# The scan of a gated delta rule: odd heads moved to the other half of the partitions, and products issued one at a time

## The chip, the cores and the metric

The kernel is one launch on 1 core of a Trainium2 chip. The metric is the device time of that launch in microseconds (us). The engines are named as the profile names them: PE is TensorE, which multiplies matrices (PEld is its loading of the stationary operand), DVE is VectorE, ACT is ScalarE, POOL is GpSimd and SP is SyncE, from whose queue all transfers (DMA) are issued. SBUF is the on-chip memory of 128 partitions; PSUM is the memory that PE writes its products to.

## The reference

One transformer block in fp32 with 1024 tokens of width 1024. Its mixer has two branches. One is a gated delta rule with 4 heads of width 128; the other is a dilated attention with 8 heads of width 64. Both go through an output projection, and then a gated feed-forward layer of width 2816 follows. What the change touches is the gated delta rule, cut here to its core:

```
kb = kc * bc[..., None]                                  # 16 chunks of 64 tokens, 4 heads
a = strict_lower(kb @ kc^T * decay)
t_inv = inverse(eye + a)
u = t_inv @ (vc * bc[..., None]);  w = t_inv @ (kb * exp(gc)[..., None])
attn = (qc @ kc^T) * decay;  q_dec = qc * exp(gc)[..., None]
k_dec = kc * exp(gc[..., -1:] - gc)[..., None];  g_end = exp(gc[..., -1])
def step(state, ...):                                    # one after the other over the 16 chunks
    v_new = u_i - w_i @ state
    o_i = q_dec_i @ state + attn_i @ v_new
    state = state * g_end_i + k_dec_i^T @ v_new
```

After the scan each head's output is normalised by its root mean square and multiplied by a gate.

## The kernel before, in words

**Stages.** PE first runs the input projections (tiles `pj`, `tp`), three fp32r products for one fp32 one: weights and activations are each split into a high and a low part, and `mm3` makes high x high, high x low and low x high. In between come the preparations of the delta rule (`post_k`, `post_q`, `intra`, `post_v`, `inverse`, `solve`). From about 281 us the scan (`chain`) runs, mixed with the rest of the input projections and with the attention (tiles `pS`, `Sr`, `tp`, `ptn`, `ptf`, `pto`, `pV`). Then come the output projection (`pw`) and the feed-forward layer (`bank`), which takes the second half of the time.

**One step of the scan.** A step is one chunk of 64 tokens for all 4 heads; two chunks c = 0 and 1 share a tile of 128 tokens t. The 64 tokens of chunk c lie in partitions 64c to 64c + 63 (`nat`), and the other half of the partitions (`sw`) holds the part of the products that gives the output. A step has three blocks of products on PE, each of four matmuls (one for each head) of 128x128 by 128 columns in fp32, and between them other engines work:

- p1: `p<-state,ckq`, the keys and queries of the chunk times the state. DVE makes `R` out of the `nat` half (four SCALAR_TENSOR_TENSOR, one a head). ACT makes `o` out of the `sw` half (`chain_o1`, four ACTIVATE), on its own time. POOL multiplies the state by its decay.
- p2: `p<-R,cg`. The matrix `cg` has 128 rows, 64 of which belong to the chunk. The other 64 meet rows of `R` that were set to zero once (a memset). ACT copies the `nat` half to `vn` (64x512), DVE adds the `sw` half to `o` (64x512).
- p3: `p<-vn,ckd`, again with 64 rows of zeros in `vn`. DVE adds it to the state (128x512).

p1 and p3 share one PSUM buffer (tag p1), p2 has another. When both chunks of a tile are done, `chain_out` normalises `o` (DVE `o<-o,on_r`), PE transposes it (`otp`) and it is written to memory (`d_mix`).

**What sets the order.** Nothing runs by hand. A planner, `Weaver`, takes generators ("strands") such as `chain`, `proj_half`, `unit` (attention) and simulates the engines with costs that stand in `Op` (lines 160 to 181): a matmul goes by its columns, an ACT instruction that reads PSUM costs 60 + 0.83 per element (+ 85 for a scale by partition), a DVE instruction 65 + 1.04 per element (+ 60 for SCALAR_TENSOR_TENSOR), and a change of the rows and columns that a matmul uses costs `SWITCH` = 120 ns. It takes whatever can start first; on PE it prefers an operation whose data were ready `MARGIN` = 850 ns before (line 399). A strand that yields a list gets it issued in one piece; `mm3` yields three products at a time. `Either` lets the planner choose an engine, with a handicap `bias` for the later ones. The instruction streams so made are fixed; on the chip every engine runs its own in order and waits on semaphores.

## Time and profile before

| | us |
|---|---|
| median of 3 runs | 1240.75 |
| lowest, highest | 1238.07, 1242.44 |
| the profiled execution, its own time | 1239.4 |
| its span, from first to last instruction | 1237.6 |
| PE busy | 1214.8 (98%) |
| DVE busy | 964.9 (78%) |
| ACT busy | 570.1 (46%) |
| POOL busy | 197.2 (16%) |

A time in the profile is one execution's; 1.35 us lie between that execution and the median of the runs, and 1.8 us between its span and its time. A fp32 matmul of the program shows as two MATMUL records. [...] How fast PE goes is read from the distance between starts.

### The profile page before, as it was taken

Reading aid. Unit: us, or ns where it says so; the run is one execution under the profiler, and the core shown is the slowest. Engines: PE = TensorE matmul, PEld = TensorE weight load, DVE = VectorE, ACT = ScalarE, POOL = GpSimd, SP = SyncE. Lnnn points to the kernel's source line nnn. Section 1 sums busy time; section 2 is a strip of 40 time slices with the busy share of each in tenths; the row PEclk is TensorE's granted clock in tenths of the full one; section 3 lists DMA queues with packets and bytes.
Section 4 is the critical chain, followed back from the end, with each engine's and each line's share of the span. In section 5 each row is a group of like instructions: output and inputs, shape, how many; then the busy total and the mean of one; then the engine's idle time right before and its main releaser. Section 6 shows DMA issues by size and latency. Waiting matters only on the chain.

```text
span 1237.6 us, 19603 instructions
## 1 busy us (share of the span) xinstructions
PE 1214.8 (98%) x6783; PEld 1015.6 (82%) x6783; DVE 964.9 (78%) x1864; ACT 570.1 (46%) x1162; POOL 197.2 (16%) x165
## 2 busy tenths in 40 slices
PE   8999999999999999999999999999999999999997
PEld 7887798888888877788788888888888888888886
DVE  5689969745999887876898867876678767976886
ACT  7535432135777667654553333333333334544541
POOL 0134321111232202110211010111001100000111
PEclk9999999999999999999999999999999999999999
DMA  8754372759887668786544444313333039645335
GB/s 272 229 158 154 111 230 78 171 188 314 243 255 226 183 182 262 236 279 196 185 136 149 143 128 128 102 61 101 119 128 118 35 104 333 246 138 150 99 123 204
DMA packets 169978, 213.42 MB, mean 172 GB/s; under 512 B 32232, under 2 KB 87016, under 8 KB 169880
## 3 DMA queue, kind: packets, MB, share of 16 engines
q1 hardware_dynamic: 169880, 212.18, 54.3%
q8 instruction: 54, 0.88, 0.3%
q14 instruction: 44, 0.36, 0.1%
HBM read 149.97 MB, written 65.95 MB: 174 GB/s over the span
## 4 chain that ended last, share of the span: by engine, by line
PE 82%; DVE 6%; DMA 5%; ACT 2%; SPq 2%; issue 1%; POOL 1%; DVEq 0%; POOLq 0%; ACTq 0%
PE bank L283 49%; PE pj L283 16%; PE pw L283 6%; PE p L283 3%; PE tp L283 3%; PE pS L283 2%; SPq L283 2%; PE pm L283 2%; PE pV L283 1%; DMA xn<-in_x 1%; DMA d_bias<-d_rev 1%; DMA y<-in_w_out 1%; DMA wor<-in_w_out 1%; DVE yc L283 0%; DMA xT<-in_x_t 0%
## 5 line engine op out<-in xcount | busy, mean ns | idle before, releaser
L283 PE MATMUL pj<-hTh,w 128*128 128x512 f32 x768 | 263.7, 402 | 5.3 <-ACT hTh L283 5.3
L283 PEld LDWEIGHTS pj<-hTh,w 128*128 128x128 f32 x768 | 145.5, 190 | 36.8 <-ACT hTh L283 5.3
L283 ACT CAST wbh<-wraw 128x512 fp32r<-128x512 f32 x130 | 80.3, 622 | 197.7 <-PE bank L283 126.1
L283 PE MATMUL pj<-hTl,w 128*128 128x512 f32 x384 | 151.3, 394 | 0.0
L283 DVE TENSOR_TENSOR wbl<-wraw,wbh 128x512 fp32r<-128x512 f32 x131 | 93.8, 718 | 29.1 <-ACT wbh L283 29.0
L283 PE MATMUL bank<-views 128*128 128x512 f32 (+1 forms) x307 | 84.8, 384 | 0.0
L283 PEld LDWEIGHTS pj<-hTl,w 128*128 128x128 f32 x384 | 72.9, 190 | 12.3 <-DVE hTl L283 0.9
L283 PE MATMUL bank<-views,dah 128*128 128x512 f32 (+1 forms) x214 | 73.5, 379 | 0.0
L283 PE MATMUL bank<-dbh,views 128*128 128x512 f32 (+1 forms) x201 | 70.3, 380 | 0.0
L283 POOL TENSOR_TENSOR m<-m,m 128x512 f32<-128x512 f32 x18 | 28.3, 1575 | 252.0 <-DVE r L283 142.1
L283 PEld LDWEIGHTS bank<-views 128*128 128x128 f32 x307 | 57.5, 188 | 11.4
L283 PE MATMUL pw<-woh,mh 128*128 128x512 f32 x128 | 52.0, 406 | 0.4 <-DVE woh L283 0.4
L283 ACT CAST w<-wr 128x512 fp32r<-128x512 f32 x53 | 32.6, 619 | 40.7 <-PE pj L283 33.5
L283 PE MATMUL pw<-wol,mh 128*128 128x512 f32 x128 | 50.1, 392 | 0.7 <-DVE wol L283 0.7
L283 PE MATMUL pw<-woh,ml 128*128 128x512 f32 x128 | 50.1, 392 | 0.0
L283 PE MATMUL bank<-dbh,dah 128*128 128x512 f32 (+1 forms) x129 | 49.1, 381 | 0.0
L283 DVE SCALAR_TENSOR_TENSOR yc<-raw,convw,yc 128x1024 f32<-128x1024 f32 x36 | 47.2, 1312 | 0.4
L283 ACT ACTIVATE Sr<-Sr,mx 128x384 f32<-128x384 f32 (+2 forms) x64 | 38.2, 598 | 19.7 <-DVE mx L283 19.4
L283 PEld LDWEIGHTS bank<-views,dah 128*128 128x128 f32 x214 | 40.0, 188 | 7.7
L283 DVE TENSOR_TENSOR m<-bank,m 128x512 f32<-128x512 f32 x44 | 30.1, 685 | 18.3 <-PE bank L283 18.3
L283 PEld LDWEIGHTS bank<-dbh,views 128*128 128x128 f32 x201 | 37.7, 188 | 7.1
L283 ACT CAST dbh<-db 128x512 fp32r<-128x512 f32 x37 | 23.0, 621 | 40.2 <-DVE db L283 22.4
(403 smaller groups left out, 3287.8 us busy)
## 6 DMA issues: line engine op xcount, KB each, us to landing
wr<-in_w_in SPq DMA_DIRECT2D x56, 256.0 KB
wraw<-in_w_gate SPq DMA_DIRECT2D x52, 256.0 KB
wraw<-in_w_up SPq DMA_DIRECT2D x52, 256.0 KB
views<-d_hid SPq DMA_DIRECT2D x47, 256.0 KB
db<-in_w_down SPq DMA_DIRECT2D x40, 256.0 KB
qs<-d_q SPq DMA_DIRECT2D x64, 128.0 KB
da<-d_hid SPq DMA_DIRECT2D x30, 256.0 KB
d_hid<-x SPq DMA_DIRECT2D x22, 256.0 KB
```

What stands on the lines that cost most here:

```text
L283: op.fn(*op.args, **op.kw)
```

## The change

Four things are done.

**Odd heads change halves.** For heads 1 and 3 the chunk's tokens are kept in the other half of the partitions: keys and queries are stored with the two chunks exchanged (`chunks_of`), `ckd`, `cbv` and `cg` are written to memory by two transfers instead of one (`store`; 8 more transfers in all), and the factors by token (`nbeg`, `egsw`) are exchanged for odd heads by one more small matmul, one ACTIVATE and one COPY. In a step, even heads then use partitions 64c and on, odd heads the other ones.

**Products with 64 rows.** p2 and p3 take only the 64 rows that count: `gg[nat[h % 2], h, :]` and `kd[nat[h % 2], h, :]`, so that heads 0 and 2 use one half of PE's rows and heads 1 and 3 the other. Even heads write one PSUM buffer, odd heads another; p2 and p3 lie in the two halves of each. The second of them is the buffer of p1 (tag p1). So `chain` now waits for `chain_o1` (priority 0 instead of 2) before it takes that buffer for p2. p1 stays as it was. The four memsets are gone. `vn`, the addition to the state and the addition to `o` are each done in two instructions of half the size, one for even and one for odd heads.

**Products singly.** `proj_half`, the output projection and the gate and up projection yield the three products of `mm3` one by one.

**POOL before DVE.** The normalisation of `o` and the sum `qf` of the attention prefer POOL; DVE gets them only where it would end more than `SPARE` = 1500 ns sooner. In the new streams POOL has all 8 of the first (none before) and 13 of 16 of the second (5 before). The planner's choices elsewhere move too: ACT has 30 instead of 22 casts to `ptf`, DVE 2 instead of 10. The planner's cost for a matmul of 64 rows to 128 columns becomes 0.87 per column (1.667 for 128 rows).

The diff, cut to its core:

```
+SPARE = 1500.0
-                c = n * 1.667 if out.shape[0] == P else ...
+                c = n * 0.87 if args[1].shape[0] == 64 and out.shape[0] == P else n * 1.667 if out.shape[0] == P else ...
...
-            yield mm3(ps[:], wh[k // 4][:, k % 4, :], wl[k // 4][:, k % 4, :], *h_of(k, hf * 512, 512),
-                      k == 0, k == KT - 1)
+            for op in mm3(ps[:], wh[k // 4][:, k % 4, :], wl[k // 4][:, k % 4, :], *h_of(k, hf * 512, 512),
+                          k == 0, k == KT - 1):
+                yield op
...
+    def store(h, dst, src):
+        if h % 2:
+            for x in (0, 64):
+                yield SY.dma_start(dst[x:x + 64], src[64 - x:128 - x])
+        else:
+            yield SY.dma_start(dst, src)
...
-        for c in range(2):
-            for z in (Rs[c], vns[c]):
-                yield G.memset(z[64 - 64 * c:128 - 64 * c, :, :], 0.0)
...
-                nat = slice(c * 64, c * 64 + 64)
-                sw = slice(64 - c * 64, 128 - c * 64)
+                nat = [slice(64 * x, 64 * x + 64) for x in (c, 1 - c)]
+                sw = nat[::-1]
...
+                    o1 = w.spawn(chain_o1(o, p1, sw, us), 0)
...
-                    w.spawn(chain_o1(o, p1, sw, us), 2)
-                p2 = yield cp.get([P, GH, P], F32, name="p2")
-                yield [mm(p2[:, h, :], gg[:, h, :], R[:, h, :]) for h in range(GH)]
+                    yield o1
+                    cp.put(p1)
+                ps = []
+                for e in range(2):
+                    z = yield cp.get([P, 2, 2, P], F32, name="p2", tag=("p2", "p1")[e])
+                    ps.append(z)
+                yield [mm(ps[h % 2][:, 0, h // 2, :], gg[nat[h % 2], h, :], R[nat[h % 2], h, :]) for h in range(GH)]
                 if not end:
-                    yield A.copy(vn[nat, :, :], p2[nat, :, :])
-                    p3 = yield cp.get([P, GH, P], F32, name="p3", tag="p1")
-                    yield [mm(p3[:, h, :], kd[:, h, :], vn[:, h, :]) for h in range(GH)]
+                    yield [A.copy(vn[nat[e], e::2, :], ps[e][nat[e], 0]) for e in range(2)]
+                    yield [mm(ps[h % 2][:, 1, h // 2, :], kd[nat[h % 2], h, :], vn[nat[h % 2], h, :]) for h in range(GH)]
...
-                        yield V.tensor_tensor(st[:], st[:], p3[:], ALU.add)
+                            yield V.tensor_tensor(st[:, e::2, :], st[:, e::2, :], ps[e][:, 1], ALU.add)
...
-        yield V.tensor_tensor(o[:], o[:], r[:].unsqueeze(2).broadcast_to([P, GH, P]), ALU.mult)
+        yield Either(*[x.tensor_tensor(o[:], o[:], r[:].unsqueeze(2).broadcast_to([P, GH, P]), ALU.mult) for x in (G, V)], bias=SPARE)
...
-        yield Either(*[x.tensor_tensor(qf[:], qs[0][:].bitcast(F32), qs[1][:].bitcast(F32), ALU.add) for x in (V, G)])
+        yield Either(*[x.tensor_tensor(qf[:], qs[0][:].bitcast(F32), qs[1][:].bitcast(F32), ALU.add) for x in (G, V)], bias=SPARE)
```

Three places of the new streams follow; a line number of L283 or L284 is that of the helper that records every instruction.

PE, second step of the scan (t = 0, c = 1), from p1 (`p<-state`) to p2 (`p<-R`), before. The `pj` rows are products of an input projection.

```order
L283 MATMUL p<-state,ckq 128x128 x4
L283 MATMUL pj<-hTh,w 128x512
L283 MATMUL pj<-hTl,w 128x512
L283 MATMUL pj<-hTh,w 128x512 x2
L283 MATMUL pj<-hTl,w 128x512
L283 MATMUL pj<-hTh,w 128x512 x2
L283 MATMUL pj<-hTl,w 128x512
L283 MATMUL pj<-hTh,w 128x512 x2
L283 MATMUL pj<-hTl,w 128x512
L283 MATMUL pj<-hTh,w 128x512
```

The same place after:

```order
L284 MATMUL p<-state,ckq 128x128 x4
L284 MATMUL pj<-hTh,w 128x512 x2
L284 MATMUL pj<-hTl,w 128x512
L284 MATMUL pj<-hTh,w 128x512 x2
L284 MATMUL pj<-hTl,w 128x512
L284 MATMUL pj<-hTh,w 128x512 x2
L284 MATMUL pj<-hTl,w 128x512
L284 MATMUL pj<-hTh,w 128x512 x2
L284 MATMUL pj<-hTl,w 128x512
L284 MATMUL pj<-hTh,w 128x512 x2
L284 MATMUL pj<-hTl,w 128x512
```

Between p1 and p2 of this step PE has 15 products instead of 12. Both pieces end right ahead of p2.

DVE, end of the third step of the scan, before (`state<-state,p` takes in p3, `o<-o,p` takes in p2; `ptn`, `pto` and ISA rows belong to the attention):

```order
L283 TENSOR_TENSOR on_r<-on_r,rqsw 128x4
L283 TENSOR_TENSOR o<-o,on_r 128x512
L283 CAST ptn<-tp 128x128
L283 TENSOR_TENSOR ptn<-tp,ptn 128x128
L283 TENSOR_TENSOR ptn<-tp,ptn 128x256
L283 TENSOR_TENSOR state<-state,p_3257 128x512
L283 TENSOR_TENSOR o<-o,p_3205 64x512
```

The same place after:

```order
L284 CAST ptn<-tp 128x128
L284 TENSOR_TENSOR ptn<-tp,ptn 128x128
L284 TENSOR_TENSOR ptn<-tp,ptn 128x256
L284 TENSOR_TENSOR state<-state,p_3203 128x2x128
L284 TENSOR_TENSOR state<-state,p_3204 128x2x128
L284 TENSOR_TENSOR o<-o,p_3204 64x2x128
L284 TENSOR_TENSOR o<-o,p_3203 64x2x128
```

The normalisation `o<-o,on_r` has left DVE, and two instructions have become four of half the size.

POOL, first steps of the scan, before (`on_r` is the factor of the normalisation; `w` and `bl` are low parts of the projections):

```order
L283 TENSOR_TENSOR state<-state,gE 128x512
L283 TENSOR_TENSOR w<-wr,w 128x512
L283 TENSOR_TENSOR qf<-qs_3029,qs_3049 128x512
L283 TENSOR_TENSOR state<-state,gE 128x512
L283 TENSOR_TENSOR on_r<-on_m,mhalf 128x4
L283 TENSOR_TENSOR state<-state,gE 128x512
```

The same place after:

```order
L284 TENSOR_TENSOR state<-state,gE 128x512
L284 TENSOR_TENSOR on_r<-on_m,mhalf 128x4
L284 TENSOR_TENSOR o<-o,on_r 128x512
L284 TENSOR_TENSOR bl<-bl,bh 128x512
L284 TENSOR_TENSOR state<-state,gE 128x512
L284 TENSOR_TENSOR qf<-qs_3244,qs_3247 128x512
L284 TENSOR_TENSOR on_r<-on_m,mhalf 128x4
L284 TENSOR_TENSOR state<-state,gE 128x512
```

The scan's own `state<-state,gE` now shares POOL with `o<-o,on_r` and with more of the `qf`.

## Rows read from the trace of the kernel before

**Rows 1.** Busy time by stage: us, each engine's busy time with its instructions in brackets, granted clock of PE (1.00 is 2.4 GHz), share and rate of the DMA engines. The stages are: up to the scan; scan; rest of the attention; output projection; feed-forward.

```profile
0.00:280.00 280.00, 272.00 (x1826) 229.47 (x1827) 209.37 (x381) 116.75 (x189) 63.87 (x53) 1.00 0.59 177
280.00:440.00 160.00, 159.12 (x1256) 138.98 (x1255) 138.40 (x425) 108.69 (x305) 38.50 (x34) 1.00 0.79 239
440.00:520.00 80.00, 74.60 (x506) 58.98 (x505) 65.27 (x193) 54.34 (x132) 14.77 (x14) 1.00 0.78 240
520.00:620.00 100.00, 98.53 (x479) 81.76 (x479) 77.44 (x134) 53.83 (x111) 14.84 (x17) 1.00 0.66 215
620.00:1237.60 617.60, 610.52 (x2724) 506.46 (x2722) 474.40 (x734) 236.51 (x425) 65.22 (x47) 1.00 0.42 138
```

**Rows 2.** Who PE waited for from 280 to 440 us, all of it: us in total, times, longest.

```profile
PE tp L283 <- DVE ptmp L283: 0.4, 1, 0.4
PE pS L283 <- DVE ptn L283: 0.3, 1, 0.3
```

**Rows 3.** The same from 440 to 520 us, the first two and the last of 7 rows, which come to 5.1 us.

```profile
PE tp L283 <- ACT Sr L283: 1.3, 2, 1.1
PE pS L283 <- DVE ptn L283: 1.1, 1, 1.1
...
PE pS L283 <- DVE ptf L283: 0.3, 1, 0.3
```

**Rows 4.** PE's groups of the scan, by form: rows*columns of PE in use, shape of the moving operand, count | busy us, mean ns of one record | idle before.

```profile
L283 PE MATMUL p<-R,cg 128*128 128x128 f32 x128 | 16.8, 274 | 0.0
...
L283 PE MATMUL p<-vn,ckd 128*128 128x128 f32 x120 | 15.8, 274 | 0.0
```

**Rows 5.** PE in order of time around the first p2: start, duration in us.

```profile
281.05 0.39 PE L283 MATMUL pj<-hTl,w 128*128 128x512 f32 x1
281.28 0.40 PE L283 MATMUL pj<-hTh,w 128*128 128x512 f32 x1
281.51 1.05 PE L283 MATMUL p<-R,cg 128*128 128x128 f32 x8
282.32 0.48 PE L283 MATMUL pj<-hTh,w 128*128 128x512 f32 x1
282.64 0.39 PE L283 MATMUL pj<-hTl,w 128*128 128x512 f32 x1
```

**Rows 6.** PE in order of time around a block that uses half of PE's columns (16 matmuls of `intra`, two halves in turn).

```profile
138.18 0.39 PE L283 MATMUL pj<-hTh,w 128*128 128x512 f32 x1
138.50 1.97 PE L283 MATMUL pm<-kq 128*64 128x128 f32 x32
140.40 0.50 PE L283 MATMUL pj<-hTh,w 128*128 128x512 f32 x1
140.73 0.40 PE L283 MATMUL pj<-hTl,w 128*128 128x512 f32 x1
```

**Rows 7.** Two stretches inside that block with the same beginning, this tile's instructions alone: columns as in rows 1, PE and PEld first.

```profile
138.90:139.05 0.15, 0.15 (x8) 0.15 (x6) 0.00 (x0) 1.00 1.14 345
138.90:140.03 1.13, 1.13 (x26) 1.13 (x24) 0.00 (x0) 1.00 1.11 375
```

**Rows 8.** Two such stretches of a block of `solve` with 64 rows, 32 columns, 32 moving columns; one matmul in the lower and one in the upper half of the rows in turn.

```profile
234.95:235.10 0.15, 0.15 (x16) 0.15 (x16) 0.00 (x0) 1.00 0.00 0
234.95:235.42 0.47, 0.47 (x36) 0.47 (x36) 0.00 (x0) 1.00 0.00 0
```

**Rows 9.** Weight loads by form: 128, 64 and 32 columns.

```profile
L283 PEld LDWEIGHTS p<-R,cg 128*128 128x128 f32 x128 | 16.5, 191 | 1.1
...
L283 PEld LDWEIGHTS pm<-kq 128*64 128x64 f32 x128 | 6.9, 137 | 1.2 <-issue 0.7 <-PE pj L283 0.4
...
L283 PEld LDWEIGHTS pm<-uz,a 64*32 64x32 f32 x128 | 2.2, 110 | 0.5 <-issue 0.5
```

**Rows 10.** DVE's groups from 280 to 520 us that the change touches, or that have the size of a new half.

```profile
L283 DVE SCALAR_TENSOR_TENSOR R<-p,nbeg,cbv 64x128 f32<-64x128 f32 x60 | 17.1, 347 | 5.8 <-PE p L283 5.6
...
L283 DVE TENSOR_TENSOR plow<-pV,plow 64x256 f32<-64x256 f32 x31 | 12.7, 411 | 9.5 <-ACT plow L283 9.3
L283 DVE TENSOR_TENSOR o<-o,p 64x512 f32<-64x512 f32 x15 | 10.2, 682 | 0.6 <-PE p L283 0.3
...
L283 DVE TENSOR_TENSOR state<-state,p 128x512 f32<-128x512 f32 x14 | 9.6, 684 | 3.0 <-PE p L283 2.7
L283 DVE TENSOR_TENSOR qf<-qs,qs 128x512 f32<-128x512 f32 x11 | 9.3, 844 | 0.5 <-DMA qs<-d_q 0.4
...
L283 DVE TENSOR_TENSOR o<-o,on_r 128x512 f32<-128x512 f32 x8 | 5.5, 686 | 0.2
...
L283 DVE CAST ptf<-tp 128x128 fp32r<-128x128 f32 x10 | 2.8, 277 | 0.0
```

**Rows 11.** ACT's groups in the same stretch.

```profile
L283 ACT ACTIVATE o<-p,egsw 64x128 f32<-64x128 f32 x60 | 17.1, 357 | 8.5 <-DVE R L283 6.3 <-DVE oss L283 1.4 <-PE pS L283 0.5
...
L283 ACT COPY plow<-pV 64x256 f32<-64x256 f32 x31 | 11.2, 361 | 7.2 <-DVE ptmp L283 4.8 <-PE pV L283 2.3
L283 ACT COPY vn<-p 64x512 f32<-64x512 f32 x15 | 8.7, 581 | 6.2 <-PE p L283 6.0
```

**Rows 12.** Chain of work, the last product of the scan and the first of the output projection: start, duration.

```profile
436.64 0.91 PE p L283 x8
...
506.53 2.36 PE pw L283 x8
```

More of the change, by code (lines that the diff above doesn't have):

```diff
@@ L163, in __init__ @@
                 n = _free(args[2])
-                c = n * 1.667 if out.shape[0] == P else 36 + 0.44 * n if n <= 64 else n * 1.0 if out.shape[0] == 64 else n * 0.45
+                c = n * 0.87 if args[1].shape[0] == 64 and out.shape[0] == P else n * 1.667 if out.shape[0] == P else 36 + 0.44 * n if n <= 64 else n * 1.0 if out.shape[0] == 64 else n * 0.45
         elif self.dma:
@@ L998, in block_kernel, with chunks_of, odd @@
     kqs = {}
+    def chunks_of(h, ap):
+        p, x, (n, _), y = [list(d) for d in ap.rearrange("p (t c j) -> p t c j", t=NT, c=2).ap]
+        return sub(ap, [p, x, [-n, 2], y], n) if h % 2 else sub(ap, [p, x, [n, 2], y])
+    def store(h, dst, src):
[4 more added lines that the diff above has]
+            yield SY.dma_start(dst, src)
+    def odd(ap):
+        return ap.rearrange("p (a b t) -> p a b t", a=2, b=2)[:, :, 1, :]
     ev_k, ev_q, ev_kq = ([Event() for _ in range(GH)] for _ in range(3))
@@ L1027, in post_k @@
         ev_k[h].fire()
-        yield SY.dma_start(d_kd[:, :, h, :].rearrange("t p d -> p t d"), kn[:])
+        yield from store(h, d_kd[:, :, h, :].rearrange("t p d -> p t d"), kn[:])
         pk.put(kn)
@@ L1093, in intra @@
                 t = 4 * b + k
-                ops += [mm(kk[0:64, k, :, :], kq[:, t, 0, :], kq[:, t, 0:2, :]),
-                        mm(kk[64:128, k, :, :], kq[:, t, 3, :], turned(kq[:, t, 2:4, :]))]
+                for c in range(2):
+                    x = c ^ h % 2
+                    r = kq[:, t, 2 * x:2 * x + 2, :]
+                    ops.append(mm(kk[64 * c:64 * c + 64, k, :, :], kq[:, t, 3 * x, :], turned(r) if x else r))
         ev_kk[h].fire()
@@ L1122, in post_v @@
         pk.put(ys)
-        yield SY.dma_start(d_bv[:, :, h, :].rearrange("t p d -> p t d"), kn[:])
+        yield from store(h, d_bv[:, :, h, :].rearrange("t p d -> p t d"), kn[:])
         pk.put(kn)
@@ L1145, in inverse @@
                   ident[32 * c:32 * c + 32, 32 * c:32 * c + 32]) for c in range(4)]
+        yield mm(rp[:, 64:96], perm[:], nbeg[:])
         rl = pv.tile([P, 32], F32, name="rl")
@@ L1148, in inverse @@
         yield V.tensor_copy(rqsw[:], rp[:, 0:32])
+        yield V.tensor_copy(odd(nbeg[:]), odd(rp[:, 64:96]))
         pm.put(rp)
@@ L1220, in solve @@
                 pm.put(gg)
-                yield SY.dma_start(d_g[4 * b:4 * b + 4, :, q, :].rearrange("t p d -> p t d"), gs[:, b])
+                yield from store(q, d_g[4 * b:4 * b + 4, :, q, :].rearrange("t p d -> p t d"), gs[:, b])
                 ev_gs[q, b].fire()
@@ L1400, in chain @@
                 if begin:
-                    yield Either(A.copy(R[nat, :, :], bv[nat, :, :]), V.tensor_copy(R[nat, :, :], bv[nat, :, :]))
+                    for e in range(2):
+                        z = R[nat[e], e::2, :], bv[nat[e], e::2, :]
+                        yield Either(A.copy(*z), V.tensor_copy(*z))
                 else:
                     p1 = yield cp.get([P, GH, P], F32, name="p1")
-                    yield [mm(p1[:, h, :], kq[:, h, 2 * c:2 * c + 2, :], st[:, h, :]) for h in range(GH)]
@@ new lines, in chain @@
+                    cp.put(p1)
+                ps = []
+                for e in range(2):
+                    z = yield cp.get([P, 2, 2, P], F32, name="p2", tag=("p2", "p1")[e])
+                    ps.append(z)
+                yield [mm(ps[h % 2][:, 0, h // 2, :], gg[nat[h % 2], h, :], R[nat[h % 2], h, :]) for h in range(GH)]
+                if not end:
+                    yield [A.copy(vn[nat[e], e::2, :], ps[e][nat[e], 0]) for e in range(2)]
+                    yield [mm(ps[h % 2][:, 1, h // 2, :], kd[nat[h % 2], h, :], vn[nat[h % 2], h, :]) for h in range(GH)]
+                    for e in range(2):
+                        if begin:
+                            yield A.copy(st[:, e::2, :], ps[e][:, 1])
+                        else:
+                            yield V.tensor_tensor(st[:, e::2, :], st[:, e::2, :], ps[e][:, 1], ALU.add)
@@ L1416, in chain @@
+                for e in (1, 0):
+                    z = o[sw[e], e::2, :]
                     if begin:
-                        yield A.copy(st[:], p3[:])
+                        yield A.copy(z, ps[e][sw[e], 0])
                     else:
-                        yield V.tensor_tensor(st[:], st[:], p3[:], ALU.add)
-                    cp.put(p3)
-                if begin:
-                    yield A.copy(o[sw, :, :], p2[sw, :, :])
-                else:
-                    yield V.tensor_tensor(o[sw, :, :], o[sw, :, :], p2[sw, :, :], ALU.add)
@@ L1425, in chain @@
-                cp.put(p2)
+                        yield V.tensor_tensor(z, z, ps[e][sw[e], 0], ALU.add)
+                    cp.put(ps[e])
             ch.put(kq, gg, kd, bv)
@@ L1448, in chain_out @@
         ot = yield ch.get([P, GH, 2, 64], F32, name="ot", bufs=1)
-        for c in range(2):
-            yield A.activation(ot[:, :, c, :], tp[:, :, 1 - c, :], AF.Copy, scale=onorm[:])
+        for e in range(2):
+            z = tp[:, e::2]
+            if not e:
+                p_, x_, (n_, _), y_ = [list(d) for d in z.ap]
+                z = sub(z, [p_, x_, [-n_, 2], y_], n_)
+            yield A.activation(ot[:, e::2], z, AF.Copy, scale=onorm[:])
         banks.put(tp)
@@ L1842, in out_proj @@
                     yield ev_wo[4 * part + k][b]
-                    yield mm3(ps[b][:], mh[:, k, :], ml[:, k, :], *(z[:, k, :] for z in wo[part, b]),
-                              part == 0 and k == 0, part == 1 and k == 3)
+                    for op in mm3(ps[b][:], mh[:, k, :], ml[:, k, :], *(z[:, k, :] for z in wo[part, b]),
+                                  part == 0 and k == 0, part == 1 and k == 3):
+                        yield op
                 if t == NT - 1:
```

20 lines of the change are left out of this document (12 added, 8 removed).

## The prediction

> **What bounds the kernel now.** I read the busy time by stage first. [...] Busy time says little for overlapped matmuls, so the second view is what PE waited for: 0.7 us in the 160 us in which the scan runs [rows 2], and 5.1 us in the next 80, nearly all on ACT and DVE [rows 3]. PE is the bound there, and the scan's long dependence from step to step is hidden behind projections and attention. The runner-up is DVE: 138.4 of 160 us in the scan's stage, 65.3 of 80 after it [rows 1]; ACT and POOL have room. So two things can move the end: PE time that the products really save, and waits that appear or go between 280 and 520 us. The feed-forward half (620 us on) has no scan in it, and its PE goes through 610.5 of 617.6 us busy; singly ordered products change nothing that PE has to do there. I cost that part at nothing; its cover is that PE never runs dry.
>
> **Products of 64 rows, the main term.** There are 16 blocks p2 and 15 blocks p3 (128 and 120 records, 8 a block) [rows 4]. What one costs now is read from starts: from the product ahead of the block to the second one behind it, 281.28 to 282.64, are 1.36 us, and the step of such a product is 0.23 [rows 5]. So a block takes 1.36 - 2 x 0.23 = 0.90 us, 8 records at 0.11, and entering and leaving it costs nothing visible.
>
> No matmul with 64 rows and 128 columns is in the trace. The nearest rows are matmuls on half of PE's columns, two halves in turn. Inside the block, the longer of two stretches with one beginning has 18 records more in 0.98 us, which is 9 pairs at 0.109 us [rows 7]: two records in the time of one. But the whole block, from 138.18 to 140.73, is 2.55 us; less two products it is 2.09, and 16 pairs account for 1.74. So 0.35 us go on entering and leaving that use of the array [rows 6]. In 64 rows a block of four matmuls is 8 records, 4 pairs: 4 x 0.109 + about 0.36 (a little more, as 128 columns of weights must be there before the first pair instead of 64) = 0.80 us. Against 0.90 that saves 0.10 us, and 31 blocks save **3.1 us**. Most of what the pairing gains is paid at the borders, because a block is so short and p1, projections or attention lie between any two.
>
> The bounds: if the change of rows alone costs nothing, a block is 0.44 us and 31 save 14.3 us. If two halves of the rows do not run together, a block is 8 x 0.11 + 0.36 = 1.25 us and 31 lose 10.9 us. I stay at 3.1, since the rows on columns show both the pairing and the border directly, and a change of rows and columns in `solve` (64 rows, 32 columns) pairs as well: 20 records in 0.32 us, a pair every 32 ns [rows 8].
>
> What could stop it are the weight loads. They last 191, 137 and 110 ns for 128, 64 and 32 columns [rows 9], some 0.85 ns more per column. So a load of 128 columns with 64 rows should keep its length (about 0.11 us of transfer), and the pair only goes at 0.109 if two loads run side by side. In rows 8 they do: 20 loads of 32 columns in 320 ns, where one after the other would need 20 x 27 = 540. There the two differ in columns as well as in rows. [...]
>
> **The two-instruction halves, and what leaves DVE.** A DVE instruction of 256 elements out of PSUM takes 411 ns, one of 512 takes 682 to 684; two halves cost 0.14 us more, and 14 + 15 splits cost DVE 4.0 us [rows 10]. Off DVE go 8 normalisations at 0.686 (5.5 us), 8 sums `qf` at some 0.69 to 0.84 (6 us) and 8 casts at 0.277 (2.2 us): 13.7 us. Net, DVE has nearly 10 us less in a stretch of 240 us where it is the runner-up. ACT gets 15 x (2 x 0.361 - 0.581) = 2.1 us for `vn` [rows 11] and about as much in casts, with 163 of 240 us busy [rows 1]; POOL gets 16 instructions, with 53 of 240 busy. Neither binds. PE itself gains only what it waited for: most of the 5.1 us of rows 3 were on DVE or on work behind DVE. I take **2 us** of gain here (0 to 5).
>
> **The new wait for `o`.** p2 now needs the buffer of p1, so `chain_o1` must be done first. On ACT, `o` waits for `R` on DVE [rows 11], so the two run one after the other: 4 x 0.347 + 4 x 0.357 = 2.82 us instead of 1.39 [rows 10, 11]. Behind the waiting p2 on PE stands everything else. The new order puts 15 products there instead of 12, 3.45 us instead of 2.76 at 0.23. That leaves 0.63 us for three hand-overs between engines, where 1.37 were left for two. The planner is too hopeful: its formulas give 0.258 us for an `R` and 0.251 for an `o`, 2.04 us for the eight, and its margin of 0.85 us is all but eaten by the missing 0.78. Likewise p1 now waits for three halves (1.23 us: both additions to the state, and the odd `o` that frees its buffer) instead of one 0.68. I put **1 us** of new waits against it (0 to 9, below). `store` adds 8 transfers on SP, the exchange one small matmul, one ACT and one DVE instruction; all lie under the 272 us in which PE works on projections [rows 1], and the scan's first `cg` comes from them. If that cover were gone they would cost 1 to 2 us once.
>
> **The sum.** Against the profiled execution: 1239.4 - 3.1 - 2 + 1 = 1235.3 us. The median lies 1.35 us above that execution, so 1236.7 us. A measurement of this kernel can tell 0.3%, 3.7 us, from no change; the forecast lies just outside.
>
> **The rivals.**
> (a) *Borders free.* If changing rows alone needs no pause, the gain is 14.3 us instead of 3.1: 1225.5 us. Against it: every change of rows or columns that I could read costs 0.3 us or more.
> (b) *No pairing.* The change doesn't do what it says: two halves of the rows run one after the other (weights, or results to two PSUM buffers), and each block still pays its borders: +10.9 - 2 + 1 gives 1250.7 us. For it: no row with equal columns. Against it: rows 7 and 8. [...]
> (c) *Waits eat it.* Place: p2 behind `o`, p1 behind the halves, 30 times. The slack that remains is some tenths of a us, ACT's queue holds instructions of 0.6 us, and DVE is 86% busy; each time that PE comes too early, nothing else can pass it. An average of 0.1 us takes the 3.1 away; from 0.2 us on it is slower than before; 0.3 us is 9 us and 1244.7 us. Against it: PE waited only 0.7 us in this stage before, with the same planner. That the scan gets longer by itself costs nothing: its last product came 69.9 us before the output projection's first [rows 12], and some 0.5 to 0.7 us in each of 15 steps is 10 us.
>
> **How the numbers follow.** Forecast as summed 0.42 (1232 to 1241); (a) 0.13; (b) 0.18; (c) 0.27 (1239 to 1248). Faster by over 0.3%: 0.27 of the forecast and all of (a), 0.40. Within 0.3%: 0.15 of the forecast and 0.15 of (c), 0.30. Slower: (b) and 0.12 of (c), 0.30. The range leaves out the better half of (a) and the worst of (b): 1227 to 1250 us.
>
> **What would show it.** In the new trace the groups `p<-R` and `p<-vn` should read 64*128, with two starts some 6 ns apart and 0.11 us to the next two; a block with two products, start to start as above, should be 1.26 us (0.90 for (a), 1.71 for (b)). Waits of PE's `p` on ACT `o` or DVE `state` between 280 and 440 us should stay near 1 us; 5 or more is (c). DVE in 280 to 520 us should fall by some 10 us, and PE's waits from 440 to 520 us from 5 to about 3. The forecast is wrong if the stretch from 0 to 280 us or from 620 us on changes by more than 2 us, which I hold to be untouched.

## The result and the profile after

The changed kernel takes 1243.85 us (median of 12 runs), the kernel before 1239.16 us beside it: a ratio of 1.0037, 95% interval 1.0029 to 1.0046. It is slower by 4.6 us, where 4.1 us less than before was forecast. Two executions far outside the rest, one here (1389.17 us, at a granted clock of 0.82) and one of halves below (3126.88 us), stand in the medians but not in the ratios. The profiled execution of the changed kernel has a span of 1241.3 us.

Busy time by stage, with the same bounds and columns as [rows 1]:

```profile
0.00:280.00 280.00, 271.26 (x1828) 228.28 (x1829) 210.83 (x385) 114.28 (x190) 58.50 (x48) 1.00 0.60 179
280.00:440.00 160.00, 156.54 (x1230) 122.36 (x1230) 135.87 (x437) 112.89 (x320) 55.11 (x48) 1.00 0.77 237
440.00:520.00 80.00, 77.14 (x524) 62.61 (x523) 64.81 (x186) 54.63 (x140) 11.49 (x13) 0.98 0.75 231
520.00:620.00 100.00, 97.29 (x466) 79.64 (x465) 71.06 (x121) 52.81 (x110) 12.74 (x18) 1.00 0.67 215
620.00:1241.30 621.30, 614.21 (x2743) 509.77 (x2741) 478.26 (x740) 240.67 (x436) 64.95 (x48) 1.00 0.42 137
```

In the scan's stage PE is busy for 156.5 of 160 us, where it was 159.1, and it does 26 records fewer in that time (1230 against 1256). DVE falls from 138.4 + 65.3 to 135.9 + 64.8 us in the two stages from 280 to 520 us: 3.0 us less, not 10.

What PE waited for from 280 to 440 us, and below it from 440 to 520 us (us in total, times, longest), as in [rows 2, 3]:

```profile
PE pS L284 <- DVE pto L284: 1.1, 1, 1.1
PE tp L284 <- ACT Sr L284: 0.7, 2, 0.4
PE tp L284 <- DVE on_r L284: 0.6, 1, 0.6
PE pS L284 <- DVE ptf L284: 0.4, 1, 0.4
PE tp L284 <- DVE on_m L284: 0.3, 1, 0.3
PE tp L284 <- DVE mx L284: 0.2, 1, 0.2
```

```profile
PE pS L284 <- issue: 2.4, 1, 2.4
PE tp L284 <- ACT Sr L284: 0.4, 1, 0.4
```

In the scan's stage 0.7 us have become 3.3; from 440 to 520 us 5.1 have become 2.8, the size that was forecast. Not one of these rows has `p` in front: in the two stages PE does not wait for the scan itself. It waits with attention's transposes and scores (`tp`, `pS`), in the scan's stage for what DVE and ACT make; for the longest wait, 2.4 us, the profile names no releaser. Only just ahead of 280 us is there a wait of the scan, with its first p2, which the kernel before does not have:

```profile
PE p L284 <- DMA ckq<-d_kq: 1.0, 1, 1.0
```

Behind the wait of 2.4 us PE's granted clock falls. The clock after its end (columns as in [rows 1]):

```profile
470.20:472.00 1.80, 1.76 (x21) 1.27 (x22) 1.74 (x5) 0.34 (x2) 0.00 (x0) 0.78 0.99 284
472.00:474.00 2.00, 2.00 (x8) 1.81 (x8) 2.00 (x12) 1.33 (x5) 0.00 (x0) 0.50 0.91 233
474.00:476.00 2.00, 2.00 (x22) 1.28 (x21) 1.27 (x5) 0.97 (x5) 1.17 (x1) 0.85 0.91 247
```

PE stood still from 467.8 to 470.2 us, and then it runs at 0.50 for part of the next 6 us: 1.8 x 0.22 + 2 x 0.50 + 2 x 0.15 = 1.7 us are lost besides. Counted with what follows it, this wait cost more than its row says; with the 1.7 us the stretch from 440 to 520 us has lost 4.5 us, hardly less than the 5.1 before.

PE's groups of the scan, by form, from 270 to 470 us (columns as in [rows 4]):

```profile
L284 PE MATMUL p<-R,cg 64*128 64x128 f32 x128 | 11.6, 297 | 1.0 <-DMA ckq<-d_kq 1.0
L284 PE MATMUL p<-vn,ckd 64*128 64x128 f32 x120 | 10.7, 297 | 0.0
```

PE in order of time around one p2, in the manner of [rows 5]:

```profile
287.31 0.39 PE L284 MATMUL pj<-hTl,w 128*128 128x512 f32 x1
287.63 0.71 PE L284 MATMUL p<-R,cg 64*128 64x128 f32 x8
288.27 0.73 PE L284 MATMUL pj<-hTh,w 128*128 128x512 f32 x2
```

The block does pair: eight records take 0.71 us instead of 1.05. By the starts of the single records the two of a pair begin 6 to 7 ns apart, as forecast; the second pair follows the first after 213 ns, the others after 112. But the block begins 0.32 us after the product ahead of it, where 0.23 was usual, and the next product begins 0.64 us after the block begins. From product to product that is 0.96 us against 1.04 (281.28 to 282.32) in [rows 5]. In the measure of the forecast, from the product ahead to the second one behind, it is 1.30 us (the second one starts at 288.61) against 1.36 before and 1.26 forecast. The median of all such blocks between projections is 1.30 against 1.35 us. An undisturbed block so takes 0.85 us instead of 0.90, 0.40 of it at its borders.

**Where PE's time went.** For every two PE records that follow one another I took the distance between starts less the undisturbed step of the first (0.227 us for 512 columns, 0.111 for a `p` record with 128 rows, 0.0555 with 64), up to the first product of the feed-forward layer (`bank`). What is over at a change of rows or columns is a border, whatever delays PE there; the rest are waits, the short ones and what a low clock costs included. Added up, in us:

| | first `bank` | steps | borders | waits | from there to the end |
|---|---|---|---|---|---|
| before | 598.6 | 560.2 | 13.4 | 19.8 | 639.0 |
| after | 603.0 | 546.6 | 26.7 | 24.4 | 638.3 |

The pairing saves 13.5 us of steps. The borders of the 64-row blocks take 13.3 us back, so that the main term is 0.2 us in this comparison. The whole loss is in the waits, 4.6 us, and 1.7 of these are the low clock after the wait at 470 us. The feed-forward part is as it was (638.3 us against 639.0).

### The profile page after: what moved, and what is told of

It reads as the page before. It is cut to its first block, busy times and chain, and to the rows that moved or that the text cites. A ratio compares the mean times of both kernels' runs of the same rounds, so it can differ in the third digit from the quotient of the medians.

```text
span 1241.3 us, 19732 instructions
## 1 busy us (share of the span) xinstructions
PE 1216.4 (98%) x6785; PEld 1002.7 (81%) x6785; DVE 960.8 (77%) x1865; ACT 575.3 (46%) x1192; POOL 202.8 (16%) x175
## 4 chain that ended last, share of the span: by engine, by line
PE 81%; DVE 10%; DMA 3%; ACT 3%; issue 2%; SPq 1%; POOL 0%; DVEq 0%; POOLq 0%; ACTq 0%
PE bank L284 49%; PE pj L284 15%; PE pw L284 6%; PE tp L284 4%; PE pS L284 2%; PE p L284 2%; PE pm L284 2%; PE pV L284 2%; DVE yc L284 2%; DVE X L284 1%; DVE tm L284 1%; DMA d_g<-gs 1%; SPq L284 1%; DVE R L284 1%; DVE w L284 1%
## 5 line engine op out<-in xcount | busy, mean ns | idle before, releaser
L284 PE MATMUL pj<-hTh,w 128*128 128x512 f32 x768 | 253.6, 402 | 5.3 <-ACT hTh L284 5.3
L284 ACT CAST wbh<-wraw 128x512 fp32r<-128x512 f32 x131 | 81.0, 621 | 203.6 <-PE bank L284 123.6
L284 PEld LDWEIGHTS pj<-hTh,w 128*128 128x128 f32 x768 | 142.4, 190 | 33.9 <-ACT hTh L284 5.8
L284 PE MATMUL pj<-hTl,w 128*128 128x512 f32 x384 | 154.5, 402 | 0.0
L284 DVE TENSOR_TENSOR wbl<-wraw,wbh 128x512 fp32r<-128x512 f32 x131 | 93.2, 714 | 29.0 <-ACT wbh L284 29.0
L284 PEld LDWEIGHTS pj<-hTl,w 128*128 128x128 f32 x384 | 72.8, 190 | 15.6 <-issue 1.4
L284 PE MATMUL bank<-views 128*128 128x512 f32 (+1 forms) x307 | 84.8, 384 | 0.0
L284 PE MATMUL bank<-views,dah 128*128 128x512 f32 (+1 forms) x214 | 73.5, 379 | 0.0
L284 PE MATMUL bank<-dbh,views 128*128 128x512 f32 (+1 forms) x201 | 70.3, 380 | 0.0
L284 POOL TENSOR_TENSOR m<-m,m 128x512 f32<-128x512 f32 x18 | 28.3, 1571 | 255.1 <-DVE r L284 142.1
L284 PEld LDWEIGHTS bank<-views 128*128 128x128 f32 x307 | 57.5, 188 | 11.5
L284 PE MATMUL pw<-woh,mh 128*128 128x512 f32 x128 | 50.7, 396 | 1.6 <-ACT mh L284 1.6
L284 PE MATMUL pw<-woh,ml 128*128 128x512 f32 x128 | 50.6, 395 | 0.2
L284 PE MATMUL pw<-wol,mh 128*128 128x512 f32 x128 | 50.7, 396 | 0.0
L284 ACT CAST w<-wr 128x512 fp32r<-128x512 f32 x51 | 31.1, 618 | 41.0 <-PE pj L284 33.0
L284 PE MATMUL bank<-dbh,dah 128*128 128x512 f32 (+1 forms) x129 | 49.1, 381 | 0.0
L284 DVE SCALAR_TENSOR_TENSOR yc<-raw,convw,yc 128x1024 f32<-128x1024 f32 x36 | 46.9, 1302 | 0.4
L284 PEld LDWEIGHTS bank<-views,dah 128*128 128x128 f32 x214 | 40.0, 188 | 7.6
L284 ACT ACTIVATE Sr<-Sr,mx 128x384 f32<-128x384 f32 (+2 forms) x64 | 38.3, 598 | 16.9 <-DVE mx L284 15.9
L284 DVE TENSOR_TENSOR m<-bank,m 128x512 f32<-128x512 f32 x44 | 30.1, 686 | 18.2 <-PE bank L284 18.2
L284 PEld LDWEIGHTS bank<-dbh,views 128*128 128x128 f32 x201 | 37.7, 188 | 7.2
L284 ACT CAST dbh<-db 128x512 fp32r<-128x512 f32 x37 | 23.0, 621 | 38.3 <-DVE db L284 22.8
```

Of the source, the lines that this page charges most:

```text
L284: op.fn(*op.args, **op.kw)
```

## The experiments

Each ratio is against the kernel before on the same chip in the same batch. "Order" below is the instruction streams that the planner makes. Where it makes a new one, it also moves some instructions that `Either` leaves open to another engine.

| run | what it is | median us | ratio, 95% interval |
|---|---|---|---|
| full_rows | after, products on 128 rows, same order | 1245.91 | 1.0047 [1.0035, 1.0059] |
| no_single | after, long products in threes | 1246.56 | 1.0047 [1.0034, 1.0060] |
| dve_first | after, DVE preferred again | 1248.57 | 1.0064 [1.0051, 1.0077] |
| no_tile | before, with single products and POOL first | 1232.93 | 0.9945 [0.9933, 0.9958] |
| only_single | before, with single products | 1238.81 | 0.9993 [0.9982, 1.0003] |
| wait_o | no_tile, p2 ordered behind `o` | 1240.97 | 1.0014 [1.0003, 1.0025] |
| halves | no_tile, `vn`, state, `o` in two halves | 1237.54 | 0.9984 [0.9973, 0.9995] |
| third_bank | after, no wait for `o` | 1255.25 | 1.0128 [1.0112, 1.0143] |
| prices_after | after, three prices corrected | 1252.37 | 1.0096 [1.0078, 1.0115] |
| prices_no_tile | no_tile, the same prices | 1244.59 | 1.0035 [1.0021, 1.0049] |
| margin_no_tile | no_tile, margin 830 | 1244.46 | 1.0038 [1.0025, 1.0051] |
| margin_after | after, margin 830 | 1243.54 | 1.0029 [1.0018, 1.0039] |
| after_m810, _m870, _m890 | after, other margins | 1241.32, 1241.89, 1241.33 | 1.0009 [0.9993, 1.0025], 1.0017 [1.0004, 1.0030], 1.0008 [0.9993, 1.0022] |
| before_m810, _m870, _m890 | before, other margins | 1238.04, 1237.95, 1240.14 | 0.9984 [0.9971, 0.9996], 0.9988 [0.9974, 1.0003], 1.0001 [0.9986, 1.0016] |

**full_rows: the same order without the pairing.** The products p2 and p3 take 128 rows again, half of them zeros; the planner is told the cost of products with 64 rows, so that the order stays that of the changed kernel. The zeros are written once, by eight memsets.

```
-  mm(ps[h % 2][:, 0, h // 2, :], gg[nat[h % 2], h, :], R[nat[h % 2], h, :])
+  as64(mm(ps[h % 2][:, 0, h // 2, :], gg[:, h, :], R[:, h, :]))
+  G.memset(z[64 * x:64 * x + 64, e::2, :], 0.0)
```

> The changed kernel with p2 and p3 on all 128 rows again (the rows of the other chunk meet rows of R and vn that are set to zero once by 8 memsets on POOL); the order of every other engine and of PE is the changed kernel's, instruction by instruction. Theory: entering and leaving 64 rows eats all that the pairing saves: in the changed kernel's trace 31 blocks save 13.5 us of PE work and pay 13.4 us at their borders, so this one lies within 1.5 us of the changed kernel, 1243 to 1245 us. Rival 1: the pairing does pay the 3 us of the prediction and waits hide it: 3 us slower, 1247. Rival 2: the borders are the whole loss: 4 to 5 us faster, 1239.

1245.91 us, 0.10% or 1.2 us above the changed kernel by the two ratios, whose intervals overlap. PE's sequence of products is the same in both traces. The account above gives steps of 560.4, borders of 14.2 and waits of 25.9 us. With the order held, pairing saves 13.8 us of steps, pays 12.6 us of borders and so nets 1.2 us, about what the times give and what 31 undisturbed blocks at 0.05 us would (1.5 us). In this order the pairing is no loss, and the loss lies in the rest of the change.

**no_single and dve_first: one part of the change undone.** The first yields the three products of a long product at a time again, the second gives DVE its old preference.

```
-            for op in mm3(...):
-                yield op
+            yield mm3(...)
```

```
-  Either(*[x.tensor_tensor(...) for x in (G, V)], bias=SPARE)
+  V.tensor_tensor(...)
```

> The changed kernel with the three products of mm3 again in one piece. Theory (the scan's rearranged step): the loss stays, 1242 to 1247 us. Rival (products singly make PE arrive too early or change the fill): as before, 1238 to 1241 us.

> The changed kernel with DVE preferred again for the normalisation of o and for qf. Theory (the scan's rearranged step): the loss stays or grows, since DVE gets some 11 us more, 1243 to 1249 us. Rival (POOL is slow at these and delays the scan's state or the attention): 1238 to 1241 us.

Both are slower than the changed kernel, so I took neither part for what loses the time; each is a single new order, and what that is worth comes below. **no_tile** is the reverse: the kernel before with these two parts and the old scan.

> The kernel before with products ordered singly and POOL preferred for the two sums, nothing else: no exchange of halves, no 64 rows, no wait for o ahead of p2. Theory: the loss comes from the rearranged step of the scan (p2 behind o, more and longer hand-overs), so this one is as fast as the kernel before, 1237 to 1241 us. Rival: singly ordered products or POOL's part cause the loss: 1242 to 1245 us.

At 1232.93 us it is faster than both kernels, by 6.8 us against the kernel before, and below what either theory expected. On its face that says that single products and POOL gain 7 us and the scan's rearrangement loses 11. I took it so, and looked for the parts of both.

**only_single** (no_tile without the preference for POOL):

> The kernel before with one edit: the three products of each long product are yielded one by one. Theory: the gain of about 7 us that singly ordered products and the preference for POOL have together comes from the single products, which give the planner smaller pieces to fit between the scan's blocks: about 1234 us, waits of PE up to the feed-forward layer near 7 us instead of 10.6. Rival: it comes from POOL taking work off DVE, and single products alone leave the time at 1239 to 1240 us.

1238.81 us, no difference from the kernel before. Single products alone do not bring the 7 us.

**wait_o and halves: two parts of the rearrangement, each alone on no_tile.** In halves the additions to the state and to `o` are split like `vn`.

```
-                    w.spawn(chain_o1(o, p1, sw, us), 2)
+                    yield w.spawn(chain_o1(o, p1, sw, us), 0)
```

```
-  A.copy(vn[nat, :, :], p2[nat, :, :])
+  [A.copy(vn[nat, e::2, :], p2[nat, e::2, :]) for e in range(2)]
```

> Single products and the preference for POOL, scan as before (1232.9 us) with one edit: p2 is not ordered until the four o of ACT have been, and these have priority 0. Theory: p2 behind o is what makes the rearranged scan lose some 13 us against 1232.9, because o stands ahead of the attention on ACT and the step gets longer: 1240 to 1246 us, the scan's last product some 15 us later than its 424 us. Rival: the wait costs under 2 us by itself (1233 to 1235 us), and the halves or the planner's new prices cause the loss.

> Single products and the preference for POOL, scan as before (1232.9 us) with one edit: vn, the addition to the state and the addition to o are two instructions each, as in the changed kernel. No wait for o. Theory (the wait does it): the halves add 4 us of DVE and 2 us of ACT time that other work covers, 1233 to 1235 us. Rival (the halves do it): the two additions to the state are on the way from p3 to the next p1, 0.14 us in 15 steps, and push the attention back on DVE: 1238 us or more.

wait_o falls into the range of its theory, halves between its two. They lie 8.0 and 4.6 us above no_tile: together about the 13 us between no_tile and full_rows. The sum is too neat. In wait_o the scan takes as long as in no_tile (147.9 and 147.7 us from the first p2 to the last), and its p2 starts 0.26 us before the last `o` ends (median of 15 steps): its buffer is not that of p1, so the edit moves only the order. What PE waited for there from 270 to 610 us begins with one wait, in the output projection:

```profile
PE pw L284 <- ACT mh L284: 4.7, 1, 4.7
```

**third_bank: the pairing without the wait.** The odd heads' buffer comes from the four that projections and attention share, and `o` keeps its old priority.

```
-  z = yield cp.get([P, 2, 2, P], F32, name="p2", tag=("p2", "p1")[e])
+  z = yield (banks.get([P, 2, 2, P], F32, name="p2") if e else cp.get([P, 2, 2, P], F32, name="p2"))
-  o1 = w.spawn(chain_o1(o, p1, sw, us), 0)
...
-  yield o1
+  w.spawn(chain_o1(o, p1, sw, us), 2)
```

> The changed kernel with one edit: the odd heads' buffer of p2 and p3 is one of the four PSUM buffers that projections and attention share, instead of p1's, so that p2 no longer waits for o, and o has its old priority 2. Theory: without the wait most of the 13 us comes back and the pairing's 1 to 2 us show: 1231 to 1237 us, if the buffer is not missed elsewhere (it is held from p2 to the addition to o, some 3 us of every 10). Rival: the halves or the 64-row borders cause the loss, and the time stays at 1243 to 1245 us; a missed buffer would show as waits of pS, tp and pj for a free buffer.

1255.25 us: a miss for both. The scan takes 181 us, and waits rise to 33.2 us in the account. That the buffer is missed elsewhere would fit but is not shown: PE's longest waits are for data of ACT and DVE (2.7 us of `tp` for `Sr`, 1.8 of `rt` for `rtok`). So this run does not price the wait.

**Prices and margins.** Two pairs of runs ask whether the planner's knowledge matters, or its order as such.

```
-  + 85 * sum(1 for x in ins if _free(x) == 1)
+  + (209 if any(x.space == PSUM for x in ins) else 85) * sum(1 for x in ins if _free(x) == 1)
-  (60 if name == "scalar_tensor_tensor" else 0)
+  (165 if name == "scalar_tensor_tensor" and any(x.space == PSUM for x in ins) else ...)
-SWITCH = 120.0
+SWITCH = 200.0
```

```
-MARGIN = 850.0
+MARGIN = 830.0
```

> The changed kernel with three prices of the planner corrected to what the trace shows from start to start: an R 0.363 us instead of 0.258, an o 0.375 instead of 0.251, a change of rows or columns 0.200 instead of 0.120. Nothing else is edited; the order moves with the prices. Theory (hopeful prices let PE arrive at attention's products before DVE and ACT have made them): waits of PE from 280 to 520 us fall from some 12 us to under 6, and the time to 1236 to 1240 us. Rival (the longer step is the cause, whatever the planner knows of it): 1241 to 1246 us. Second rival (any new order of the same work moves the time by several us either way): no better told by prices than by the margin below.

> Single products and the preference for POOL, scan as before (1232.9 us), with the same three prices corrected. Theory of the prices: 1229 to 1233 us, since PE waits there only 7 us. Rival of new orders: anywhere from 1231 to 1240 us.

> A control: the changed kernel with the planner's margin at 830 ns instead of 850. It computes the same with the same instructions, and only their order differs. If the order alone moves the time by little, 1242 to 1246 us. If any new order moves it by several us, it lands outside, and differences of that size between other kernels here say nothing of their edits.

> The same control on single products and preference for POOL with the scan as before (1232.9 us): 1231 to 1235 us if order alone moves little, as far as 1239 us if it moves much. With the control on the changed kernel it gives the spread against which the 11 us between the two are to be held.

Right prices do not help the changed kernel in this one order: 1252.37 us, far from the 1236 to 1240 us of the theory. (In prices_no_tile, 1244.59 us and outside both expectations, they are not right: R and `o` go every 0.264 and 0.251 us there, see below.) margin_after stays where it was, at 1243.54 us. The control on no_tile is the surprise. 20 ns of margin, the same work in another order, move it from 1232.93 to 1244.46 us. The expectations call these the same instructions; not all of them are on the same engine: among others, two casts to `ptf` and two to `pto` go from ACT to DVE. What PE waited for from 280 to 605 us, first in no_tile (the first two of 7 rows), then with the other margin (all):

```profile
PE tp L284 <- DVE y L284: 1.3, 2, 1.0
PE tp L284 <- DVE pto L284: 0.9, 1, 0.9
...
```

```profile
PE pw L284 <- ACT mh L284: 4.5, 1, 4.5
PE pS L284 <- DVE pto L284: 2.0, 1, 2.0
PE pV L284 <- DVE gst L284: 1.2, 1, 1.2
PE pS L284 <- DVE on_r L284: 0.9, 1, 0.9
```

The same `pw` wait for `mh` as in wait_o, without wait_o's edit. The clock adds as much. Both kernels from 440 to 520 and from 520 to 604 us (columns as in [rows 1]), no_tile and then the other margin:

```profile
440.00:520.00 80.00, 76.93 (x496) 61.37 (x495) 63.11 (x168) 48.83 (x118) 11.93 (x12) 1.00 0.80 241
520.00:604.00 84.00, 83.63 (x402) 69.17 (x401) 61.53 (x105) 44.04 (x93) 14.78 (x17) 1.00 0.67 213
```

```profile
440.00:520.00 80.00, 72.32 (x475) 59.29 (x474) 61.83 (x177) 48.55 (x125) 11.34 (x11) 0.96 0.76 237
520.00:604.00 84.00, 84.00 (x402) 69.48 (x401) 54.12 (x96) 38.48 (x81) 7.80 (x13) 0.98 0.61 194
```

With the other margin, which has waits of 2.0 and 4.5 us, PE is at 0.50 for a time, and the means of 0.96 and 0.98 cost 80 x 0.04 + 84 x 0.02 = 4.9 us; no_tile has 1.00 in both stretches. So no_tile was a lucky order, and differences of 5 or 8 us between single orders say nothing of an edit: the verdicts on wait_o and halves are withdrawn, and so is the 7 us gain. For the same reason no_single, dve_first, only_single and prices_after, one order each, acquit or convict no part of the change.

**Three more orders of either kernel.** That leaves the loss of the change itself in doubt. The margin of 830 ns leaves the streams of the kernel before as they are, so its further orders are those with 810, 870 and 890 ns.

> The kernel before with the planner's margin at 810 ns instead of 850: the same instructions in another order. If the order as such moves the time by several us, as on single products, the three orders of the kernel before spread over some 1233 to 1245 us and overlap those of the changed kernel. If the rearranged step is what costs, they stay near 1239 us.

> The same with 870 ns: 1233 to 1245 us if order decides, near 1239 us if not.

> The same with 890 ns: 1233 to 1245 us if order decides, near 1239 us if not.

> The changed kernel with the margin at 810 ns: the same instructions in another order. With 1243.9 us (850 ns) and 1243.5 us (830 ns) on record, order alone would give some 1236 to 1250 us here, as often below the orders of the kernel before as above them; a cost of the rearranged step keeps it at 1243 us or above.

> The changed kernel with the margin at 870 ns: some 1236 to 1250 us if order decides, 1243 us or above if the rearranged step costs by itself.

> The same with 890 ns: some 1236 to 1250 us if order decides, 1243 us or above if the rearranged step costs by itself.

Four orders of the kernel before lie at 0.9984 to 1.0001 (mean 0.9993), five of the changed kernel at 1.0008 to 1.0037 (mean 1.0020). The groups do not overlap, so these nine orders speak for a cost of the change itself, some 0.27% or 3.3 us on average. It is not proof: single intervals of the two groups do overlap, nine orders are few, and the three new ones of the changed kernel (1241.3 to 1241.9 us) lie below the 1243 us that the expectations had set for such a cost. The order that the change came with is the slowest of its five; the other four lie within 0.3% of the kernel before. PE's account over the same profiles:

| mean us (lowest to highest) | steps | borders | waits | to the end |
|---|---|---|---|---|
| before, 4 orders | 560.2 | 13.4 | 19.3 (16.5 to 21.1) | 639.9 (639.0 to 641.0) |
| after, 5 orders | 546.6 | 27.4 | 21.4 (18.3 to 24.4) | 640.0 (638.3 to 645.3) |

Steps and borders nearly cancel again (+0.5 us), and waits are 2.1 us more. Of these, 1.2 us are the clock. Before the first `bank`, PE runs at 0.50 for 0, 0, 6.8 and 0 us in the four orders before (850, 810, 870, 890 ns), and for 3.4, 6.8, 3.4, 6.8 and 0 us in the five after (850, 810, 870, 890, 830 ns); half of that is lost, 0.85 us against 2.04 on average. Each of these stretches begins late in or shortly after a wait of PE of 1.6 to 3.9 us, but margin_after has a wait of 2.2 us and no fall. The mean granted clocks of all executions differ the same way (0.997 after, 0.998 before). In margin_after the order helps the attention (18.3 us of waits) and spoils the start of the feed-forward layer, so that the rest takes 645.3 us.

**What the rearranged step costs DVE and ACT.** The traces have one more thing that no forecast named. Groups of DVE and ACT in the changed kernel, from 270 to 540 us (busy us, mean ns of one):

```profile
L284 DVE SCALAR_TENSOR_TENSOR R<-p,nbeg,cbv 64x128 f32<-64x128 f32 x60 | 21.0, 350 | 8.9 <-PE p L284 4.2 <-ACT o L284 3.8
L284 DVE TENSOR_TENSOR o<-o,p 64x256 f32<-64x256 f32 x30 | 12.5, 417 | 0.6
L284 DVE TENSOR_TENSOR state<-state,p 128x256 f32<-128x256 f32 x28 | 10.5, 415 | 2.9 <-PE p L284 2.8
L284 ACT ACTIVATE o<-p,egsw 64x128 f32<-64x128 f32 x60 | 21.8, 363 | 6.3 <-DVE R L284 5.0 <-PE p L284 0.5
L284 ACT COPY vn<-p 64x256 f32<-64x256 f32 x30 | 11.0, 366 | 0.9 <-PE p L284 0.4
```

The same groups in halves, where all heads of a chunk lie in the same 64 partitions:

```profile
L284 DVE SCALAR_TENSOR_TENSOR R<-p,nbeg,cbv 64x128 f32<-64x128 f32 x60 | 17.2, 349 | 0.8 <-PE p L284 0.6
L284 DVE TENSOR_TENSOR o<-o,p 64x256 f32<-64x256 f32 x30 | 11.3, 414 | 0.2
L284 DVE TENSOR_TENSOR state<-state,p 128x256 f32<-128x256 f32 x28 | 10.5, 415 | 6.1 <-PE p L284 5.9
L284 ACT ACTIVATE o<-p,egsw 64x128 f32<-64x128 f32 x60 | 17.2, 356 | 10.2 <-DVE R L284 7.2 <-DVE on_m L284 3.0
L284 ACT COPY vn<-p 64x256 f32<-64x256 f32 x30 | 9.6, 368 | 2.8 <-PE p L284 2.5
```

One R lasts as long (350 and 349 ns), but sixty of them keep DVE busy for 21.0 us instead of 17.2. Busy time counts overlap once: in halves one begins before the last has ended, in the changed kernel, where heads in turn lie in the lower and the upper 64 partitions, it does not. Median distances between starts in a row: R 264 and 371 ns, `o` 251 and 375, `vn` 269 and 391. The addition to `o` has 329 to 345 ns and 436 to 456. The addition to the state, which takes all 128 partitions, has 338 and 334 (medians). third_bank, where p2 does not wait for `o`, has the longer distances too (R 371, `o` 374), so they come with the alternating halves and not with the wait. It is so on DVE (264 against 371 ns) and on ACT (251 against 375); what in the engines makes the difference is not shown. In the sums of busy time it is 3.8 + 1.2 us on DVE and 4.6 + 1.4 us on ACT, and it lies in the step:

```profile
325.56 1.17 DVE L284 SCALAR_TENSOR_TENSOR R<-p,nbeg,cbv 64x128 f32<-64x128 f32 x4
```

is the four R of a step in halves (start, duration of the four), and of one in the changed kernel:

```profile
343.06 1.46 DVE L284 SCALAR_TENSOR_TENSOR R<-p,nbeg,cbv 64x128 f32<-64x128 f32 x4 [0.23 <-ACT o L284]
```

ACT's four `o` of that step, in the changed kernel:

```profile
341.54 1.49 ACT L284 ACTIVATE o<-p,egsw 64x128 f32<-64x128 f32 x4
```

Here `o` comes first and R has to wait for it. With priority 0 the planner of the submitted order does so in 10 of 15 steps; with margins of 810, 830 and 870 ns R comes first in 10 or 11 and p2 follows `o`. The median time from p1's first product to p2's is the same in both cases, 4.8 to 5.0 us, against 3.74 in the kernel before.

## Why the prediction was wrong

**The main term, products of 64 rows.** The mechanism was right in both its parts, and the size was off. Pairs go every 0.111 us (0.109 forecast) with equal columns, and rival (b) is out. The border was taken at 0.36 us from half columns [rows 6]; in an undisturbed block it is 0.40. The account has 14.4 us for 31 blocks (mean of five orders), 0.47 us each, with the waits that fall on a border, such as the 1.0 us at the first p2. A block is then 4 x 0.111 + 0.47 = 0.91 us, what it was. Of the 3.1 us, 1.5 are left by undisturbed blocks, 1.2 by full_rows, none by the mean over orders. Rival (a) is out.

**What leaves DVE.** This step failed. The splits were priced at 4.0 us by size and all instructions by their durations, while the exchange of partitions took the overlap from R (371 ns from start to start instead of 264), from `o` (375 instead of 252) and from the halves of `vn` and of the addition to `o`. The forecast did not weigh it, and its rows [rows 10, 11], with all of a row in the same partitions, did not show it. DVE got 3.0 us less in 280 to 520 us instead of nearly 10. What left it was as forecast (14.2 us against 13.7). On it came 2.0 us for the splits, as halves has them, and 5.0 us for the lost overlap, which was priced at nothing; and the planner gave it three `wol` that POOL had made before (1.7 us). The rest are other moves of the planner. The gain in waits came from 440 to 520 us (2.3 us) and was lost in the scan's stage (2.6 us) and, by the same list, from 520 to 640 us (2.6 instead of 1.5 us).

**"The planner is too hopeful."** Wrong as argued. I held its 0.258 and 0.251 us against durations of 0.347 and 0.357. In a row the next one starts before the last has ended: in the kernel before every 0.264 and 0.252 us, and by that the planner was right. Only the change made it wrong, and in the one order of prices_after telling it so did not help.

**The new wait for `o`.** The forecast of a serial 2.82 us was near (1.46 + 1.49 and 0.03 between them, medians of the submitted order), but by luck: it added durations, which overlapped in the kernel before (four R in 1.17 us), and only the lost overlap that it did not foresee made the sum come out. That the scan gets longer by 0.5 to 0.7 us a step was near too: from the first p2 to the last it takes 167.5 us instead of 155.7, 0.8 us a step. The place was wrong: past the first step, with its wait of 1.0 us for a transfer, PE of the submitted order does not wait with p2 or p1. Its waits are with attention's products, whose makers, DVE and ACT, are the ones that the step holds longer; that this is why is argued, not shown.

**The sum.** For waits 2 - 1 = 1 us of gain was forecast; they came out 4.6 us worse in the submitted order and 2.1 us worse on average over orders, 1.7 and 1.2 of it by a lower clock, for which the sum had no term. That is rival (c) in its time (1244.7 us) and not in its place. Missing altogether was the spread of orders. It is as large as the terms of the sum: 1.7 thousandths within the kernel before, 2.9 within the changed one, 9 between two orders of no_tile.

**What stays open.** What makes the waits longer is not shown: the lost overlap, p2's wait for `o`, POOL's part or the orders themselves. wait_o and halves have neither the alternating halves nor the shared buffer, and each is a single order. A kernel that takes the heads as 0, 2, 1, 3, so that only one R and one `o` of a step change halves, was not run. no_tile at 1232.93 us is the fastest kernel here, faster than both; by its control that belongs to its order.

## What to carry to other kernels

Where a planner sets the order, measure an edit in several orders of the same work before pricing it: here 20 ns of a margin moved a kernel by 11.5 us, and two neat experiments had to be withdrawn. Price DVE and ACT instructions in a row by the distance between starts, and keep such a row in the same partitions: an R went every 0.264 us there and every 0.371 in alternating halves, an `o` every 0.252 and 0.375. Hold what pairing on halves of the rows saves in a block against the border that it adds: here four pairs at 0.111 us saved 0.45 us of eight steps and paid 0.40 us and more. By these two numbers, an estimate, a block of twice the length would keep about half of what it saves.

## What was not expected of the hardware

- In the kernel before, an R (DVE) or `o` (ACT) that follows another in the same 64 partitions starts 0.08 or 0.10 us before the last one ends (medians); in the changed kernel, where they alternate between the lower and the upper 64, it starts 0.01 to 0.02 us after it (distances of R 264 against 371 ns, of `o` 252 against 375). Sixty R keep DVE busy for 17.1 us before and 17.2 in halves and wait_o, for 21.0 in the changed kernel and 20.9 in third_bank.
- In the changed kernel two matmuls with 64 rows and 128 columns each, in different halves of the rows and with two PSUM buffers, start 6 to 7 ns apart in most blocks and keep a pair every 111 to 112 ns, except that the second pair of a block comes 213 ns after the first.
- In the changed kernel, to go into such a block and out again cost 0.40 us undisturbed and 0.47 us on average over its five orders, more than the 0.35 us of half columns [rows 6].
- After a wait of 2.4 us PE ran at a granted clock of 0.50 for 3.4 us, which cost another 1.7 us. Between two orders of no_tile the lower clock was worth 4.9 of 11.5 us.
